# The block sums of the 7-product down chunks on GpSimd, and a seventh such chunk

## The chip, the cores and the metric

The kernel runs on one NeuronCore of a Trainium2 chip. The metric is the device time of one execution in microseconds (us), the median of three runs. All engines that the text names belong to that core: TensorE (PE; its weight loads stand apart as PEld), VectorE (DVE), ScalarE (ACT), GpSimd (POOL) and SyncE (SP), whose queue issues the loads.

## What is computed

One decoder layer for 256 tokens of width 1024: an input projection, two groups of eight attention heads, an output projection, a layer norm, a SwiGLU feed-forward part of inner width 2816, and a second layer norm. The change lies in the last product, the down projection. In the reference:

```
h = _layer_norm(ALPHA * h + mix_out, ln1_g[l], ln1_b[l])
gate = jnp.einsum('bsd,df->bsf', h, w_gate[l])
up = jnp.einsum('bsd,df->bsf', h, w_up[l])
ffn = jnp.einsum('bsf,fd->bsd', jax.nn.silu(gate) * up, w_down[l])
h = _layer_norm(ALPHA * h + ffn, ln2_g[l], ln2_b[l])
```

## The kernel before

Every matmul works on float32 numbers cut in two parts, hi and lo: `split` lets ACT write the rounded hi part and DVE write lo = source - hi. `prod` then issues three matmuls (hi*hi, hi*lo, lo*hi). So each weight has to pass ACT and DVE before PE can use it. Weights come in chunks of 128x2048 (1 MB) through four buffers `wraw`, loaded by SP; the parts lie in five buffers each of `whi` and `wlo` (a pair is called a unit here). `Weights.piece` issues the next piece of this work, and the order on each engine is the order in which the program issues it: an engine that waits holds up all that stands behind it.

The 22 feed-forward tiles (f = 0 to 21) each write a PSUM tile `pg`; after the last of them comes the down projection. It has 11 chunks of two f tiles each, worked through in the order of the table `DOWN`. An ordinary chunk needs one unit, and PE makes 8 products of 512 columns with it (24 matmuls). A chunk in `FAST` is computed as a 2x2 block product with 7 products in place of 8 (21 matmuls), in the manner of Strassen and Winograd. For that it needs two units: A, from the weights as loaded (a 512-column and a 1024-column split), and B, from sums of the weight blocks (two 1024-column splits). The sums are made in place in `wraw` by lines 144, 145 and 146 between the splits of A and those of B: 1024, 512 and 512 columns, each step needing the one before. Of the 7 products the first three use A (PSUM tiles d1, d2, d3), the other four B (d4, d5, d7, d6). The activations of such a chunk need sums of their own (lines 608 to 611, buffer `slots`), and one split of 896 columns.

The last three chunks of `DOWN` are ordinary ones and are worked through in `finish`, token block by token block, so that the layer norm of the first 128 tokens (`layer_norm`, lines 546 to 563, buffer `y`) runs under the matmuls of the second. Ahead of it DVE adds the PSUM tiles of the 7-product chunks together (lines 732 to 743).

Of the kernel before, what the change touches and what calls it, by code (L numbers as in the profile page):

```python
# [10 lines left out]
F32 = mybir.dt.float32  # L11
# [23 lines left out]
NSPLIT = 5  # L35
NWARM = 10

DOWN = (4, 5, 0, 6, 7, 1, 8, 9, 2, 3, 10)
FAST = (4, 5, 6, 7, 8, 9)
ALPHA = 2.0 ** 0.25  # L40
SCALE = DH ** -0.5
LN_EPS = 1e-5
# [5 lines left out]
def decoder_layer(ctx: ExitStack, tc: tile.TileContext, first, x, wqk, wv, wo, wgu, wd,  # L48
                  gmix, lnrows, biases, out):
    nc = tc.nc  # L50
# [24 lines left out]
    def bank(tag, name):  # L75
        return ps.tile([128, 512], F32, tag=tag, name=name)

    def split(src, hi, lo):
        act_e.activation(hi, src, AF.Copy)
        dve.tensor_sub(lo, src, hi)  # L80

    class Weights:
# [51 lines left out]
        def sums(self, c):  # L134

            r = self.raw[c]
            parts = self.parts[c]
            if self.at == 0:
                for k in (slice(0, 512), slice(1024, 2048)):
                    split(r[:, k], parts[0][0][:, k], parts[0][1][:, k])  # L140
                self.at = 512
            elif self.at == 512:
                b = r.rearrange("p (i n) -> p i n", i=4)
                nc.vector.tensor_sub(b[:, 0:2, :], b[:, 1:4:2, :], b[:, 0:2, :])
                nc.vector.tensor_sub(b[:, 3, :], b[:, 3, :], b[:, 0, :])
                nc.vector.tensor_sub(b[:, 2, :], b[:, 2, :], b[:, 3, :])
                self.at = 1024
            else:
                if self.at == 1024:
                    if self.full():  # L150
                        return False
                    parts.append(self.unit())
                o = (self.at - 1024) * 2
                k = slice(o, o + 1024)
                split(r[:, k], parts[1][0][:, k], parts[1][1][:, k])
                self.at += 512
            return True
# [47 lines left out]
    for h in range(2):  # L205
# [3 lines left out]
    weights = Weights([wv[0, 0], wv[0, 1], wqk[0], wqk[1], wv[1, 0], wv[1, 1], wqk[2], wqk[3], wqk[4], wqk[5],  # L209
                       *(wo[c] for c in range(4)), *(wgu[f] for f in range(NFF)), *(wd[c] for c in DOWN)],  # L210
                      [14 + NFF + i for i, c in enumerate(DOWN) if c in FAST])
    weights.load(1)
# [10 lines left out]
    def prod(dst, lhs, rhs, start, stop):  # L223

        pe.matmul(dst, lhs[0], rhs[0], start=start, stop=False, skip_group_check=True)
        pe.matmul(dst, lhs[0], rhs[1], start=False, stop=False, skip_group_check=True)
        pe.matmul(dst, lhs[1], rhs[0], start=False, stop=stop, skip_group_check=True)
# [305 lines left out]
    ff = ctx.enter_context(tc.tile_pool(name="ff", bufs=3, reuse_waits="tile"))  # L533
# [53 lines left out]
    def act_tiles(f):  # L587
        if f < NPAIR:
            act[f] = tuple(cst.tile([128, S], F32R, tag=f"m{f}{i}", name=f"a{i}{f}") for i in range(2))
        else:  # L590
            act[f] = tuple(ff.tile([128, S], F32R, name=f"a{i}{f}", bufs=1) for i in range(2))

    def gated(g, u, shape, tag, dst=None):
        s = ff.tile(shape, F32, tag=tag, name="silu", bufs=3)
        nc.scalar.activation(s, g, AF.Silu)
        if dst is None:
            dst = s
        else:
            s, u = (v.rearrange("p (t n) -> p t n", t=2) for v in (s, u))
        nc.vector.tensor_mul(dst, s, u)  # L600
        return dst


    slots = {}

    def fast_sums(c):
        q = slots.pop(c)
        nc.vector.tensor_add(q[:, 3, :], q[:, 7, :], q[:, 2, :])
        nc.vector.tensor_sub(q[:, 4, :], q[:, 3, :], q[:, 0, :])
        nc.vector.tensor_sub(q[:, 5, :], q[:, 0, :], q[:, 7, :])  # L610
        nc.vector.tensor_sub(q[:, 6, :], q[:, 1, :], q[:, 4, :])  # L611
        fast_act[c] = tuple(ff.tile([128, 7, 128], F32R, name=f"s{i}{c}", bufs=1) for i in range(2))
        split(q[:, 0:7, :], *fast_act[c])
# [21 lines left out]
    def ff_by_channel(f, tag):  # L635
        w = weights.get(14 + f, 1024)
        c, odd = divmod(f, 2)
        fast = c in FAST
        if not fast:
            act_tiles(f)  # L640
        elif not odd:
            slots[c] = ff.tile([128, 8, 128], F32, tag="slots", name="slots", bufs=1)
        p = bank(tag, "pg")
        for half in range(2):
            for kt in range(KT):
                k = slice(kt * 256 + half * 128, kt * 256 + half * 128 + 128)
                od.fill(0.33, lambda: prod(p[:, half * 256:half * 256 + 256], (w[0][:, k], w[1][:, k]),
                                           (xhi[:, kt, :], xlo[:, kt, :]), kt == 0, kt == KT - 1))
        weights.free(14 + f)
        dst = None if not fast else slots[c][:, 1:3, :] if odd else slots[c][:, 0:8:7, :]  # L650
        a = gated(p[:, 0:256], p[:, 256:512], [128, 256], "aw", dst)
        if not fast:
            split(a, *act[f])
        elif odd:
            fast_sums(c)
# [22 lines left out]
    for f in range(NX, NFF):  # L678
        if f == NFF - 8:
            od.pace = 0.9  # L680
        ff_by_channel(f, ("in", "sml")[f % 2])
# [29 lines left out]
    base = 14 + NFF  # L711
    for n, c in enumerate(DOWN[:-nlast]):
        w = weights.get(base + n, 1024)
        if c in FAST:
            sh, sl = fast_act[c]
# [12 lines left out]
    y = ff.tile([128, D], F32, tag="y", name="y", bufs=1)  # L728
# [15 lines left out]

    wl = {c: weights.get(base + len(DOWN) - nlast + n, 1024) for n, c in enumerate(DOWN[-nlast:])}
    pr[9] = bank("big", "d9")
# [82 lines left out]
```

## Time and profile before

| | |
|---|---|
| median of 3 runs | 317.19 us (317.07 to 317.55) |
| profiled execution, its own time | 316.86 us |
| its span, first to last instruction | 315.1 us |
| PE busy | 305.9 us (97%) |
| DVE busy | 240.6 us (76%) |
| ACT busy | 190.7 us (61%) |
| POOL busy | 4.1 us (1%) |
| mean granted TensorE clock | 0.996 |

The span leaves out 1.76 us that lie around it in the profiled execution. Busy shares are means over the whole program; the stage that the change touches is the stretch from about 225 us to 299 us of the span, and the rows further down are taken from there.

### The profile page before, as it was taken

To read this page: it belongs to the slowest core of one execution; us is meant where nothing else is said; L and a number is where in the kernel's file an instruction comes from. 1 tells how busy PE (TensorE), PEld (TensorE's weight loads), DVE (VectorE), ACT (ScalarE), POOL (GpSimd) and SP (SyncE) were. 2 spreads that over 40 slices of the span, in tenths; PEclk is the share of its full clock that TensorE was granted. 3 is DMA by queue.
4 is the path that set the end of the run, shared out by engine and by line. 5 is a ranking of instruction groups with operands and counts; after the bars stand their busy time and mean duration, and the time that the engine had idled before them with its cause. 6 is when DMAs were issued, how large, how long until landed. Compare 5 with 4: busy or idle time off the path is not lost.

```text
span 315.1 us, 5440 instructions
## 1 busy us (share of the span) xinstructions
PE 305.9 (97%) x2112; PEld 277.8 (88%) x2112; DVE 240.6 (76%) x465; ACT 190.7 (61%) x406; POOL 4.1 (1%) x22
## 2 busy tenths in 40 slices
PE   8999999999999999999999999999999999999990
PEld 4988898799997778999999999999999988888880
DVE  4778998659897479997646466585597699999765
ACT  5789997777787458666446364473542675565011
POOL 5000000000000000000000000000000000000000
PEclk9999999999999999999999999999999999999998
DMA  7979887297332104789455464563613253630011
GB/s 255 399 301 381 277 283 263 113 358 292 151 137 69 64 2 133 249 294 370 157 189 214 139 226 172 166 235 133 218 50 136 80 188 130 270 135 0 0 67 67
DMA packets 9657, 58.02 MB, mean 184 GB/s; under 512 B 1184, under 2 KB 1440, under 8 KB 3360
## 3 DMA queue, kind: packets, MB, share of 16 engines
q1 hardware_dynamic: 9344, 57.22, 49.8%
q10 hardware_dynamic: 288, 0.46, 0.4%
q8 instruction: 16, 0.26, 0.3%
q14 instruction: 9, 0.07, 0.1%
HBM read 56.63 MB, written 1.05 MB: 183 GB/s over the span
## 4 chain that ended last, share of the span: by engine, by line
PE 94%; DVE 2%; ACT 1%; DMA 1%; issue 0%; DVEq 0%
PE pg L71 40%; PE p_in L71 22%; PE d L71 15%; PE acc L71 7%; PE z L71 2%; PE o L370 1%; PE s L71 1%; PE warm L185 1%; PE z L311 1%; DVE y L563 1%; PE o L375 1%; DVE bst L548 1%; DMA out_h<-y 1%; DVE y L546 1%; PE o L388 1%; PE tr L575 1%
## 5 line engine op out<-in xcount | busy, mean ns | idle before, releaser
L71 DVE TENSOR_TENSOR wlo<-wraw,whi 128x512 fp32r<-128x512 f32 (+2 forms) x194 | 138.0, 739 | 37.9 <-ACT whi L71 37.0
L71 ACT ACTIVATE whi<-wraw 128x512 fp32r<-128x512 f32 (+2 forms) x194 | 121.2, 671 | 58.0 <-PE pg L71 35.2
L71 PE MATMUL pg<-xhi,whi 128*128 128x256 f32 x304 | 85.7, 282 | 0.0
L71 PE MATMUL pg<-xlo,whi 128*128 128x256 f32 x304 | 85.5, 281 | 0.0
L71 PE MATMUL pg<-xhi,wlo 128*128 128x256 f32 x304 | 85.5, 281 | 0.0
L71 PEld LDWEIGHTS pg<-xhi,whi 128*128 128x128 f32 x304 | 57.2, 188 | 0.0
L71 PEld LDWEIGHTS pg<-xlo,whi 128*128 128x128 f32 x304 | 57.2, 188 | 0.0
L71 PEld LDWEIGHTS pg<-xhi,wlo 128*128 128x128 f32 x304 | 57.2, 188 | 0.0
L71 PE MATMUL p_in<-xhi,whi 128*128 128x256 f32 x128 | 36.5, 286 | 0.0
L71 PE MATMUL p_in<-xhi,wlo 128*128 128x256 f32 x128 | 36.3, 283 | 0.0
L71 PE MATMUL p_in<-xlo,whi 128*128 128x256 f32 x128 | 36.1, 282 | 0.0
L71 PE MATMUL d<-whi,s 128*128 128x512 f32 x84 | 26.9, 395 | 0.0
L71 PE MATMUL d<-whi,a 128*128 128x512 f32 (+1 forms) x92 | 25.9, 363 | 0.0
L71 PEld LDWEIGHTS p_in<-xhi,whi 128*128 128x128 f32 x128 | 24.1, 188 | 1.4 <-issue 0.7
L71 PEld LDWEIGHTS p_in<-xlo,whi 128*128 128x128 f32 x128 | 24.1, 188 | 0.2
L71 PEld LDWEIGHTS p_in<-xhi,wlo 128*128 128x128 f32 x128 | 24.1, 188 | 0.1
L71 PEld LDWEIGHTS d<-whi,s 128*128 128x128 f32 x84 | 15.8, 188 | 3.8
L71 PEld LDWEIGHTS d<-whi,a 128*128 128x128 f32 x92 | 16.6, 189 | 2.9
L71 PE MATMUL d<-wlo,a 128*128 128x512 f32 (+1 forms) x46 | 16.7, 363 | 0.0
L71 PE MATMUL d<-wlo,s 128*128 128x512 f32 x42 | 16.6, 395 | 0.0
L71 ACT ACTIVATE s<-slots 128x896 fp32r<-128x896 f32 x6 | 5.7, 953 | 13.4 <-DVE slots L611 13.4
L71 PE MATMUL pg<-wlo,xhi 128*128 128x256 f32 x48 | 13.6, 286 | 0.0
(151 smaller groups left out, 473.7 us busy)
## 6 DMA issues: line engine op xcount, KB each, us to landing
wraw<-in_wgu SPq DMA_DIRECT2D x22, 1024.0 KB, 4.8
wraw<-in_wd SPq DMA_DIRECT2D x11, 1024.0 KB, 4.8
wraw<-in_wqk SPq DMA_DIRECT2D x6, 1024.0 KB, 5.7
wraw<-in_wo SPq DMA_DIRECT2D x4, 1024.0 KB, 4.7
wraw<-in_first SPq DMA_DIRECT2D x8, 384.0 KB, 6.3
wraw<-in_wv SPq DMA_DIRECT2D x3, 1024.0 KB, 5.4
rows<-in_lnrows SPq DMA_DIRECT2D x2, 1024.0 KB, 6.6
wraw<-in_wv SPq DMA_DIRECT2D x2, 512.0 KB, 7.0
```

Source lines behind the costliest of these rows:

```text
L71: return lambda *a, **k: tc.keep_in_program_order(f(*a, **k)) if Pinned.on else f(*a, **k)
L185: nc.tensor.matmul(warm.rearrange("p (r n) -> p r n", r=4), idle, idle[:, None, :].to_broadcast([128, 4, 128]), start=True, stop=True, ski ...
L311: nc.tensor.matmul(dst, lhs, rhs, start=False, stop=True, skip_group_check=True)
L370: nc.tensor.matmul(o[r, 0:256], vt[g, 0][:, c], w0[:, h * 256:h * 256 + 256], start=True, stop=False, skip_group_check=True)
L375: nc.tensor.matmul(o[r, 128:256], vt[g, 1][:, c], w1[:, h * 128:h * 128 + 128], start=False, stop=True, skip_group_check=True)
L388: nc.tensor.matmul(ms, blkr, sq[:, i, :], start=i == 0, stop=i == 1, skip_group_check=True)
L546: nc.vector.scalar_tensor_tensor(y[:, c], res[:, c], scale, acc[i][:, :c.stop - c.start], op0=ALU.mult, op1=ALU.add)
L548: nc.vector.bn_stats(st[:, i, :], y[:, c])
L563: nc.vector.scalar_tensor_tensor(dst[:, c], y[:, c], r[:, 3:4], b[:, c], op0=ALU.mult, op1=ALU.add)
L575: nc.tensor.transpose(p[:, i * 128:i * 128 + 128], h[:, kt * 128:kt * 128 + 128], ident)
```

## The change

The table of chunks takes one chunk more into the 7-product form (chunk 10, f tiles 20 and 21), and the order of the chunks is another one: the last three are now 1, 2 and 3. The three sums of weight blocks are issued on GpSimd. The buffer in which the activations' sums are made gets the tag of the layer norms' `y`, so that the two share one place.

```diff
-DOWN = (4, 5, 0, 6, 7, 1, 8, 9, 2, 3, 10)
-FAST = (4, 5, 6, 7, 8, 9)
+DOWN = (4, 5, 6, 0, 7, 8, 9, 10, 1, 2, 3)
+FAST = (4, 5, 6, 7, 8, 9, 10)
...
-                nc.vector.tensor_sub(b[:, 0:2, :], b[:, 1:4:2, :], b[:, 0:2, :])
-                nc.vector.tensor_sub(b[:, 3, :], b[:, 3, :], b[:, 0, :])
-                nc.vector.tensor_sub(b[:, 2, :], b[:, 2, :], b[:, 3, :])
+                nc.gpsimd.tensor_sub(b[:, 0:2, :], b[:, 1:4:2, :], b[:, 0:2, :])
+                nc.gpsimd.tensor_sub(b[:, 3, :], b[:, 3, :], b[:, 0, :])
+                nc.gpsimd.tensor_sub(b[:, 2, :], b[:, 2, :], b[:, 3, :])
...
-            slots[c] = ff.tile([128, 8, 128], F32, tag="slots", name="slots", bufs=1)
+            slots[c] = ff.tile([128, 8, 128], F32, tag="y", name="slots", bufs=1)
```

On DVE, at the first 7-product chunk (chunk 4, `wraw_2708`, units `whi_2871` and `whi_2908`), where the feed-forward tiles f = 17 and 18 are still under way:

```order
 L71 TENSOR_TENSOR wlo_2872<-wraw_2708,whi_2871 128x512
 L600 TENSOR_TENSOR slots_2687<-silu_2823,pg_2758 128x256
-L144 TENSOR_TENSOR wraw_2708<-wraw_2708 128x1024
 L608 TENSOR_TENSOR slots_2687<-slots_2687 128x128
 L71 TENSOR_TENSOR wlo_2872<-wraw_2708,whi_2871 128x1024
 L609 TENSOR_TENSOR slots_2687<-slots_2687 128x128
-L145 TENSOR_TENSOR wraw_2708<-wraw_2708 128x512
 L611 TENSOR_TENSOR slots_2687<-slots_2687 128x128
-L146 TENSOR_TENSOR wraw_2708<-wraw_2708 128x512
 L71 TENSOR_TENSOR s18_2831<-slots_2687,s08_2830 128x896
```

The three sums are gone from DVE's order; the splits and the activations' sums stay in the same order.

On POOL, where nothing stood after the constants of the first 5 us, there are now three rows for each of the seven chunks. These are the ones of chunks 7, 8 and 9 (`wraw_2923`, `wraw_3053`, `wraw_3149`):

```order
L144 TENSOR_TENSOR wraw_2923<-wraw_2923 128x1024
L145 TENSOR_TENSOR wraw_2923<-wraw_2923 128x512
L146 TENSOR_TENSOR wraw_2923<-wraw_2923 128x512
L144 TENSOR_TENSOR wraw_3053<-wraw_3053 128x1024
L145 TENSOR_TENSOR wraw_3053<-wraw_3053 128x512
L146 TENSOR_TENSOR wraw_3053<-wraw_3053 128x512
L144 TENSOR_TENSOR wraw_3149<-wraw_3149 128x1024
L145 TENSOR_TENSOR wraw_3149<-wraw_3149 128x512
L146 TENSOR_TENSOR wraw_3149<-wraw_3149 128x512
```

On ACT, in the second half of the down projection. Before, the splits of chunk 8 (`wraw_3139`), chunk 9 (`wraw_3156`) and the ordinary chunk 2 (`wraw_3194`):

```order
L71 ACTIVATE whi_3249<-wraw_3139 128x512
L71 ACTIVATE whi_3249<-wraw_3139 128x1024
L71 ACTIVATE whi_3258<-wraw_3139 128x1024
L71 ACTIVATE whi_3287<-wraw_3156 128x512
L71 ACTIVATE whi_3258<-wraw_3139 128x1024
L71 ACTIVATE whi_3287<-wraw_3156 128x1024
L71 ACTIVATE whi_3296<-wraw_3156 128x1024
```

and now, those of chunk 8 (its end, `wraw_3053`), chunk 9 (`wraw_3149`) and chunk 10 (`wraw_3157`):

```order
L71 ACTIVATE whi_3218<-wraw_3053 128x1024
L71 ACTIVATE whi_3227<-wraw_3053 128x1024 x2
L71 ACTIVATE whi_3259<-wraw_3149 128x512
L71 ACTIVATE whi_3259<-wraw_3149 128x1024
L71 ACTIVATE whi_3289<-wraw_3149 128x1024 x2
L71 ACTIVATE whi_3297<-wraw_3157 128x512
L71 ACTIVATE whi_3297<-wraw_3157 128x1024
L71 ACTIVATE whi_3327<-wraw_3157 128x1024 x2
```

Before, the first piece of chunk 9 stood ahead of the last piece of chunk 8's second unit. Now each chunk's first piece stands behind the last piece of the one before; the same holds for DVE's part of the splits. Only chunks 7 and 8 are still issued in turns.

## Rows read from the trace of the kernel before

**Rows 1.** The page, its span, its engines (1) and its final chain (4).
```profile
span 315.1 us, 5440 instructions
...
PE 305.9 (97%) x2112; PEld 277.8 (88%) x2112; DVE 240.6 (76%) x465; ACT 190.7 (61%) x406; POOL 4.1 (1%) x22
...
PE 94%; DVE 2%; ACT 1%; DMA 1%; issue 0%; DVEq 0%
```
**Rows 2.** Waits of PE, all: who for whom, total us, times, longest.
```profile
PE warm L185 <- DVE idle L182: 1.1, 1, 1.1
PE o L370 <- ACT w L359: 0.2, 1, 0.2
```
**Rows 3.** Windows: length, then each engine's busy us.
```profile
225.00:250.00 25.00, 25.00 (x213) 25.00 (x212) 18.57 (x29) 10.25 (x15) 0.00 (x0) 1.00 0.25 86
250.00:290.00 40.00, 40.00 (x175) 32.41 (x174) 37.95 (x40) 26.49 (x30) 0.00 (x0) 1.00 0.42 158
```
**Rows 4.** Timeline of PE: start, duration; first matmuls of chunks 4, 0 and 6.
```profile
250.04 0.39 PE L71 MATMUL d<-whi,s 128*128 128x512 f32 x1
...
259.83 0.40 PE L71 MATMUL d<-whi,a 128*128 128x512 f32 x1
...
265.30 0.40 PE L71 MATMUL d<-whi,s 128*128 128x512 f32 x1
```
**Rows 5.** Groups by shape on DVE and ACT, 250 to 290 us.
```profile
L71 DVE TENSOR_TENSOR wlo<-wraw,whi 128x1024 fp32r<-128x1024 f32 x22 | 26.0, 1220 | 2.9 <-ACT whi L71 2.8
L144 DVE TENSOR_TENSOR wraw<-wraw 128x1024 f32<-128x1024 f32 x4 | 4.9, 1220 | 0.0
...
L71 DVE TENSOR_TENSOR wlo<-wraw,whi 128x512 fp32r<-128x512 f32 x4 | 2.7, 684 | 0.0
...
L71 ACT ACTIVATE whi<-wraw 128x1024 fp32r<-128x1024 f32 x22 | 22.3, 1053 | 14.3 <-DVE wraw L144 8.2 <-PE pg L71 2.8 <-PE d L71 1.8
L71 ACT ACTIVATE whi<-wraw 128x512 fp32r<-128x512 f32 x4 | 2.5, 625 | 0.0
L683 ACT ACT_TABLE_LOAD x1 | 1.3, 1283 | 0.0
```
**Rows 6.** Window with the activations' sums of one chunk on DVE and ACT.
```profile
238.70:246.10 7.40, 2.36 (x5) 0.95 (x1) 1.00 0.33 134
```
**Rows 7.** Timeline of DVE: the end of the splits and the layer norm's first instructions.
```profile
281.10 9.17 DVE L71 TENSOR_TENSOR wlo<-wraw,whi 128x1024 fp32r<-128x1024 f32 x8
290.18 0.68 DVE L732 SCALAR_TENSOR_TENSOR x_nat<-x_nat,d 128x512 f32<-128x512 f32 x1
290.78 0.68 DVE L736 TENSOR_TENSOR y<-y,d 128x512 f32<-128x512 f32 x1
...
296.15 0.69 DVE L548 BATCH_NORM_STATS2 bst<-y 128x6 f32<-128x512 f32 x1
298.86 0.69 DVE L546 SCALAR_TENSOR_TENSOR y<-x_nat,d 128x512 f32<-128x512 f32 x1 [2.02 <-PE d L71]
```
**Rows 8.** Timeline of POOL, its writes and its copies.
```profile
1.65 0.20 POOL L202 MEMSET negones<- 128x128 f32 x1
1.80 0.29 POOL L201 CAST identb<-ident 128x128 bf16<-128x128 f32 x1
2.04 0.29 POOL L203 TENSOR_SCALAR_AFFINE_SELECT negtri<-negones 128x128 fp32r<-128x128 f32 x1
...
3.28 0.53 POOL L248 MEMSET padlo<- 128x512 f32 x1
3.75 0.53 POOL L247 MEMSET padhi<- 128x512 f32 x1
...
4.78 0.09 POOL L404 MEMSET newton<- 128x1 f32 x1
```
**Rows 9.** Timeline of DVE, its first split, and another one.
```profile
4.82 0.43 DVE L71 TENSOR_TENSOR xlo<-wraw,xhi 128x256 fp32r<-128x256 f32 x1 [3.83 <-ACT xhi L71]
...
5.84 0.42 DVE L71 TENSOR_TENSOR xlo<-wraw,xhi 128x256 fp32r<-128x256 f32 x1
```

## The prediction

> **What bounds the kernel now.** I read the page first. PE is busy for 305.9 of 315.1 us, and the chain that ended last runs 94% on PE [rows 1]. The list of PE's waits says how far that goes: two waits in the whole program, 1.3 us together, both near its start and none in the down projection [rows 2]. So there each matmul follows the last, and the reader is to see how little room there is behind that: in the windows DVE is busy for 37.95 of the 40 us from 250 to 290, ACT for 26.49 and POOL for none [rows 3]. DVE delivers the weights' lo parts only just ahead of PE. The last look is at the tail: DVE's last split ends at 290.2, then it works through its additions, and it waits 2.02 us for PE before the layer norm's instruction at 298.86 [rows 7]. That wait is the slack of the whole chain of splits: a last split that ends more than 2.02 us later than 290.18 delays the layer norm, and with it the end.
>
> **What a 7-product chunk saves.** Chunk 4 starts on PE at 250.04 and the next but one, ordinary chunk 0, at 259.83: two chunks of 21 matmuls take 9.79, one 4.90. Chunk 0 with its 24 takes until 265.30, that is 5.47 [rows 4]. One more 7-product chunk ahead of `finish` thus saves PE 0.57 us (0.18% of the time), and it is the most that the change can bring, because nothing after the chunks becomes shorter: `finish` has three ordinary chunks as before. 0.2%, or 0.63 us, is about what a measurement of this kernel can tell from no change.
>
> **What it takes off DVE.** Six chunks lose 1.22 + 0.68 + 0.68 us of sums on DVE [rows 5] (a 512-column sum costs what the 512-column split does). The new 7-product chunk adds 1536 columns of splits to ACT and DVE. DVE alone becomes less loaded.
>
> **What GpSimd takes for the sums.** No row shows a two-tensor operation on POOL. Its starts bound one [rows 8]: a write of 128 columns takes 0.15 to the next start and one of 512 takes 0.47, so 0.86 ns per column and 0.03 of fixed cost. A copy or select that reads one tensor takes 0.24 for 128 columns, 1.64 ns per column; a second tensor read adds as much again as the first did, which gives 2.4. A chunk has 2048 columns in three instructions: 1.85 us at the pace of a write, 3.45 at that of a copy, 5.0 with two reads. I take 4.5, between the copy and the two reads and nearer to the two reads, because a subtraction has two. That is 1.9 us longer than on DVE, and the three sums depend on each other, so nothing divides them. A sentence by itself: the Trainium skill (GPSIMD Engine Reference, section 3.1) gives 4497 ns for a two-tensor operation of 2048 columns, by which the estimate would be the same 4.5.
>
> **Who waits for them.** ACT's splits for unit B wait for the sums, behind these on ACT stand the next chunk's first split, and behind their DVE halves the next chunk's too; PE waits at the fourth product of a chunk (d4, the first from B). Once chunks 9 and 10 are reached, no piece of the next chunk lies ahead of the last piece of the current one, so the whole round lies on the path. The loads are not late: a raw buffer is free when the chunk four before it is split (chunk 6 for chunk 9), some 20 us ahead. The shared buffer of `y` and `slots` costs nothing: the first norm has let go of it long before tile f = 8, and the second's `y` is wanted only after the last split. Chunk 10's activations add a split of 0.95 on ACT and 2.36 of busy time on DVE [rows 6] just after 250 us, in place of ordinary splits.
>
> **Whether the two engines work at the same time.** This decides the size. The one place in the trace where they meet is at 4.8 us: a DVE split of two tensors in SBUF took 0.43 while POOL's last writes ran, against 0.42 a little later [rows 8, 9]. But there POOL only wrote; that it may read two tensors while DVE also reads two is shown nowhere. I cost both ends: side by side without loss, and strictly in turns. I take the turns, the nearer to what the change asks of them (both read the very same `wraw` tile, chunk by chunk), and keep the other for the range. Weighed against the trace: the Trainium skill (SBUF — State Buffer, section "Who interferes with whom") says that a DVE instruction with two SBUF inputs contends with a GpSimd instruction that reads SBUF, not with one that only writes, and that the later one blocks until the first is done. By that rule the turns hold and the time is the 333.5 below; the rows at 4.8 us agree with its second half, and no row here shows the first.
>
> **The sum, in turns.** Starts on DVE lie 0.08 before the last end (eight splits of 1.22 in 9.17 [rows 7]), so a 1024-column split counts 1.14, a 512-column one 0.60, and the activations' five 1.94. Unit A of chunk 6 can start when the last feed-forward tile is done, at 250.04 [rows 4]; ACT's half takes 0.63 [rows 5], and DVE, with the end of chunk 5's split still to do, reaches it at about 252.0. From there DVE has five 7-product chunks (0.60 + 3 x 1.14 = 4.02 each, 20.1), chunk 10's activations (1.9) and four ordinary chunks (8 x 1.14 = 9.1): 31.1. POOL has five chunks of 4.5: 22.5. In turns that is 53.6. In chunks 6, 9 and 10 neither has anything to do while ACT splits the last block, 1.05 [rows 5] each: 3.2. The last split ends at 252.0 + 53.6 + 3.2 = 308.8, which is 18.6 after 290.18; less the slack of 2.02 the layer norm starts 16.6 later. The saving of 0.57 doesn't count then, since DVE sets the end. 316.86 + 16.6 = **333.5 us** for an execution like the profiled one. The median of the runs lay 0.33 above that one, so I forecast **333.8**. At 5.0 for a chunk's sums, with bubbles in chunks 7 and 8 too, it would be 338; at 3.45 some 328.
>
> **Rivals.** *Side by side* (slower too, by less). Chunk 6's sums end at 256.1; ACT then does in order a block of 1.05, the activations' 0.95, the table load of 1.28, chunk 0's two blocks and chunk 7's first [rows 5, 6], with DVE 1.8 behind: 263.6. The sums of chunks 7 and 8 follow one another, until 273.3. A round of chunk 9 or 10 is ACT 1.05, DVE 1.14 and 0.69, the sums 4.5 and some 0.2 of hand-over: 7.6, against the 4.90 that PE needs. 288.5, then 1.05 and seven splits of 1.14: 297.6, 7.4 late, 5.4 over the slack: 322.3, with the 0.33 322.6. For it: DVE's own load falls, and nothing in the trace shows the two engines in each other's way. *Part of each*, a DVE that only slows down while POOL reads: between 323 and 333.
>
> *Hidden* (the other side). If the two work side by side and a chunk's sums cost little, the splits stay ahead of PE and only the 0.57 remains: 316.6 by the median. Four chunks' sums (7 to 10) lie on the chain, so it decides at 4.5 - (5.4 + 0.6) / 4 = 3.0 us a chunk, below what the copies' pace gives (3.45) and above that of the writes (1.85). Against it speaks that a subtraction reads more than a copy does.
>
> **How the numbers follow.** In turns 0.50; side by side 0.27; part of each 0.13; hidden 0.10. The range leaves out the hidden case, the dearest turns and the cheapest of side by side: 321 to 337.5. Hidden lands at -0.18%, within 0.2% more often than beyond it: faster 0.03, same 0.08, slower 0.89.
>
> **What would show it.** In the profile after: PE waits in the down projection, on the splits' `whi` and `wlo`, growing from chunk 7 on and largest at the fourth product of chunks 9 and 10; ACT's idle time ahead of `whi` released by POOL's `wraw`; POOL starts of L144 and L145 some 2.2 and 1.1 apart. In turns, DVE's 1024-column splits that meet a sum last longer than 1.22 (or sums longer than 2.3), and hardly a moment has both busy to the full; side by side they keep their 1.22. DVE goes straight from its last split into the additions and no longer waits 2.02 ahead of L546. The forecast is wrong if PE has no waits there, if the splits keep 1.22 under the sums, or if L144 on POOL is far from 2.2.

## The result and the profile after

The changed kernel takes 336.06 us (median of 4 runs, 335.90 to 336.14) against 317.25 us for the kernel before (median of 4, 317.07 to 317.55): a ratio of 1.0592, 95% interval 1.0578 to 1.0605. It is 18.8 us slower. The forecast was 333.8 with a range of 321 to 337.5. The time alone doesn't say whether the two engines worked in turns; the rows do.

The page of the kernel after, its span and busy times:

```profile
span 334.4 us, 5467 instructions
...
PE 311.6 (93%) x2109; PEld 280.2 (84%) x2109; DVE 242.1 (72%) x452; ACT 192.5 (58%) x407; POOL 46.0 (14%) x43
```

Against [rows 1] the span has grown by 19.3 us. DVE lost 13 instructions and is busy for longer. That is the first sign: part of what is counted as busy there must be something else.

PE's waits after, from 225 us on (who for whom, total us, times, longest). In [rows 2] there was none in this stretch.

```profile
PE d L71 <- ACT whi L71: 8.0, 3, 3.7
PE d L71 <- DVE wlo L71: 4.5, 4, 2.5
```

The timeline of POOL after (start, duration): the sums of chunk 4, those of chunk 9 and the first of chunk 10.

```profile
229.27 2.39 POOL L144 TENSOR_TENSOR wraw<-wraw 128x1024 f32<-128x1024 f32 x1 [224.39 <-DVE wlo L71]
233.09 1.28 POOL L145 TENSOR_TENSOR wraw<-wraw 128x512 f32<-128x512 f32 x1 [1.43 <-DVE wlo L71]
234.45 1.30 POOL L146 TENSOR_TENSOR wraw<-wraw 128x512 f32<-128x512 f32 x1
...
285.73 3.32 POOL L144 TENSOR_TENSOR wraw<-wraw 128x1024 f32<-128x1024 f32 x1 [3.03 <-DVE wlo L71]
289.13 1.29 POOL L145 TENSOR_TENSOR wraw<-wraw 128x512 f32<-128x512 f32 x1
290.49 2.12 POOL L146 TENSOR_TENSOR wraw<-wraw 128x512 f32<-128x512 f32 x1
295.65 3.29 POOL L144 TENSOR_TENSOR wraw<-wraw 128x1024 f32<-128x1024 f32 x1 [3.03 <-DVE wlo L71]
```

And the timeline of DVE after, at the same places and at the end of the splits:

```profile
229.55 2.25 DVE L608 TENSOR_TENSOR slots<-slots 128x128 f32<-128x128 f32 x1
231.73 1.21 DVE L71 TENSOR_TENSOR wlo<-wraw,whi 128x1024 fp32r<-128x1024 f32 x1
232.87 0.28 DVE L609 TENSOR_TENSOR slots<-slots 128x128 f32<-128x128 f32 x1
...
283.83 2.96 DVE L71 TENSOR_TENSOR wlo<-wraw,whi 128x1024 fp32r<-128x1024 f32 x3 [3.64 <-ACT whi L71]
290.18 1.32 DVE L71 TENSOR_TENSOR wlo<-wraw,whi 128x1024 fp32r<-128x1024 f32 x1 [3.39 <-ACT whi L71]
293.74 2.96 DVE L71 TENSOR_TENSOR wlo<-wraw,whi 128x1024 fp32r<-128x1024 f32 x3 [2.24 <-ACT whi L71]
...
303.62 8.03 DVE L71 TENSOR_TENSOR wlo<-wraw,whi 128x1024 fp32r<-128x1024 f32 x7 [2.24 <-ACT whi L71]
311.58 0.68 DVE L732 SCALAR_TENSOR_TENSOR x_nat<-x_nat,d 128x512 f32<-128x512 f32 x1
...
318.15 0.67 DVE L546 SCALAR_TENSOR_TENSOR y<-x_nat,d 128x512 f32<-128x512 f32 x1
```

The two lists are to be read side by side.

*DVE waits for POOL.* L608 adds 128 columns. Its neighbour L609, of the same shape, takes 0.28 at 232.87. L608 starts at 229.55, while POOL's L144 runs (229.27 to 231.66), and ends at 231.80, a moment after it. Nothing connects the two: L608 reads activations, L144 weights. The time for which it was held up is counted in its duration, not as idle time.

*POOL waits for DVE.* L144 takes 2.39 at 229.27, alone, and 3.32 at 285.73. There DVE's last of three splits was under way, from 285.57 (286.79 less its 1.22), and ended 1.06 after L144's start. L146 takes 2.12 at 290.49, under the split of 290.18, in place of 1.29.

So whichever starts second stands until the first is done, in both directions. The Trainium skill (SBUF — State Buffer, section "Who interferes with whom") states it so, for a DVE instruction with two SBUF inputs against a GpSimd one that reads SBUF; these rows agree. L600, one of whose inputs (`pg`) lies in PSUM, is not held up: at 240.49 it takes 0.41, as before, and L144, which starts under it at 240.65, takes its 2.39.

*The round.* From L144 of chunk 9 to that of chunk 10 pass 9.92 us (285.73 to 295.65), where PE needs 4.90 for such a chunk [rows 4]. They divide so: the three sums until 292.61; ACT's last block until 293.7; DVE's splits until 295.57. ACT's timeline after, in that round:

```profile
289.08 1.06 ACT L71 ACTIVATE whi<-wraw 128x1024 fp32r<-128x1024 f32 x1 [3.82 <-POOL wraw L144]
292.65 2.52 ACT L71 ACTIVATE whi<-wraw 128x1024 fp32r<-128x1024 f32 x3 [2.50 <-POOL wraw L146]
```

The row of 292.65 holds chunk 9's last block and, behind it, the first pieces of chunk 10. They don't need the sums, but stand behind them in ACT's order, so nothing of the next chunk overlaps with the sums of this one.

*The end.* The last split ends where L732 starts, at 311.58 against 290.18 [rows 7]. L546 at 318.15 no longer waits. 311.58 - 290.18 - 2.02 = 19.4: the whole growth of the span.

### The profile page after: what moved, and what is told of

Same layout as the page of the kernel before. It is cut to its first block, busy times and chain, and to the rows that moved or that the text cites. A ratio compares the mean times of both kernels' runs of the same rounds, so it can differ in the third digit from the quotient of the medians.

```text
span 334.4 us, 5467 instructions
## 1 busy us (share of the span) xinstructions
PE 311.6 (93%) x2109; PEld 280.2 (84%) x2109; DVE 242.1 (72%) x452; ACT 192.5 (58%) x407; POOL 46.0 (14%) x43
## 3 DMA queue, kind: packets, MB, share of 16 engines
HBM read 56.63 MB, written 1.05 MB: 172 GB/s over the span
## 4 chain that ended last, share of the span: by engine, by line
PE 69%; DVE 11%; POOL 8%; ACT 4%; DMA 4%; issue 2%; POOLq 1%; DVEq 0%; ACTq 0%
PE pg L71 37%; PE p_in L71 17%; PE acc L71 7%; DVE wlo L71 5%; POOL wraw L144 3%; POOL wraw L145 2%; DMA wraw<-in_wv 2%; POOL wraw L146 2%; ACT whi L71 2%; PE z L71 2%; PE o L370 1%; PE s L71 1%; PE z L311 1%; DMA wraw<-in_first 1%; DVE bst L548 1%
## 5 line engine op out<-in xcount | busy, mean ns | idle before, releaser
L71 DVE TENSOR_TENSOR wlo<-wraw,whi 128x512 fp32r<-128x512 f32 (+2 forms) x196 | 142.9, 757 | 57.0 <-ACT whi L71 56.2
L71 ACT ACTIVATE whi<-wraw 128x512 fp32r<-128x512 f32 (+2 forms) x196 | 122.9, 672 | 74.9 <-PE pg L71 32.5
L144 POOL TENSOR_TENSOR wraw<-wraw 128x1024 f32<-128x1024 f32 x7 | 19.4, 2777 | 248.3 <-DVE wlo L71 248.3
L71 PE MATMUL d<-whi,s 128*128 128x512 f32 x98 | 34.8, 431 | 8.0 <-ACT whi L71 8.0
L71 PEld LDWEIGHTS d<-whi,s 128*128 128x128 f32 x98 | 20.7, 211 | 14.2 <-ACT whi L71 9.3
L71 PE MATMUL d<-wlo,s 128*128 128x512 f32 x49 | 21.9, 446 | 4.5 <-DVE wlo L71 4.5
L71 PE MATMUL d<-whi,a 128*128 128x512 f32 (+1 forms) x76 | 20.7, 356 | 0.0
L71 PEld LDWEIGHTS d<-wlo,s 128*128 128x128 f32 x49 | 10.3, 211 | 8.3 <-DVE wlo L71 5.9
L71 ACT ACTIVATE s<-slots 128x896 fp32r<-128x896 f32 x7 | 6.7, 951 | 16.4 <-DVE slots L611 16.4
L71 PEld LDWEIGHTS d<-whi,a 128*128 128x128 f32 x76 | 13.6, 189 | 2.1
```

Source lines behind the costliest of these rows:

```text
L71: return lambda *a, **k: tc.keep_in_program_order(f(*a, **k)) if Pinned.on else f(*a, **k)
L144: nc.gpsimd.tensor_sub(b[:, 0:2, :], b[:, 1:4:2, :], b[:, 0:2, :])
```

## The experiments

Two things had to be settled: how much of the 18.8 us comes from GpSimd at all, and whether that share is the sums' greater length, or that the two engines exclude each other. Each ratio is to the kernel before, in runs on the same chip (medians 317.17 in the first set, e1, e2, e4 and e6, and 317.53 in the second), with its 95% interval.

**e1_seven_on_dve**: the changed kernel with the sums back on DVE.

```diff
-                nc.gpsimd.tensor_sub(b[:, 0:2, :], b[:, 1:4:2, :], b[:, 0:2, :])
-                nc.gpsimd.tensor_sub(b[:, 3, :], b[:, 3, :], b[:, 0, :])
-                nc.gpsimd.tensor_sub(b[:, 2, :], b[:, 2, :], b[:, 3, :])
+                nc.vector.tensor_sub(b[:, 0:2, :], b[:, 1:4:2, :], b[:, 0:2, :])
+                nc.vector.tensor_sub(b[:, 3, :], b[:, 3, :], b[:, 0, :])
+                nc.vector.tensor_sub(b[:, 2, :], b[:, 2, :], b[:, 3, :])
```

> The change with the block sums back on DVE (the seventh 7-product chunk, the new order and the shared buffer stay). If the loss comes from GpSimd (its length and the turns), nearly all of it goes: DVE has one 7-product chunk more (4.0 of splits, 2.6 of sums and 1.9 for the activations in place of 2.3 and 0.7, so some 5.5 us more work, less the idle time it has before 250 us and the 2.0 of slack), 1.5 to 3.5 us above the kernel before, 318.7 to 320.7. The rival, that the new order and the extra chunk by themselves break the flow of the splits, expects it near the changed kernel, 330 or more.

Measured 319.88, ratio 1.0084 (1.0069 to 1.0099). PE has no wait in the down projection, as before, and still the kernel is slower. The timeline of DVE in this kernel shows why:

```profile
286.46 9.17 DVE L71 TENSOR_TENSOR wlo<-wraw,whi 128x1024 fp32r<-128x1024 f32 x8
295.55 0.68 DVE L732 SCALAR_TENSOR_TENSOR x_nat<-x_nat,d 128x512 f32<-128x512 f32 x1
...
302.12 0.67 DVE L546 SCALAR_TENSOR_TENSOR y<-x_nat,d 128x512 f32<-128x512 f32 x1
```

The seventh chunk gives DVE more to split and add. Its last split ends 5.37 us after that of before [rows 7]; less the slack of 2.02 that is 3.35, and the span grew by 3.3. The seventh chunk with its order costs 2.7 by the medians; the other 16 us need GpSimd. They hold a change of order too: in e1 ACT and DVE still take the first piece of chunk 9 ahead of the last piece of chunk 8, and that of chunk 10 ahead of the last of chunk 9, which the change does not.

**e2_six_on_pool**: the kernel before, with only lines 144 to 146 on GpSimd.

```diff
-                nc.vector.tensor_sub(b[:, 0:2, :], b[:, 1:4:2, :], b[:, 0:2, :])
-                nc.vector.tensor_sub(b[:, 3, :], b[:, 3, :], b[:, 0, :])
-                nc.vector.tensor_sub(b[:, 2, :], b[:, 2, :], b[:, 3, :])
+                nc.gpsimd.tensor_sub(b[:, 0:2, :], b[:, 1:4:2, :], b[:, 0:2, :])
+                nc.gpsimd.tensor_sub(b[:, 3, :], b[:, 3, :], b[:, 0, :])
+                nc.gpsimd.tensor_sub(b[:, 2, :], b[:, 2, :], b[:, 3, :])
```

> The kernel before with nothing changed but the engine of the block sums: six chunks, the old order. In turns: POOL's 5.0 us for each of chunks 6 to 9 come on top of DVE's splits, 20 us in place of the 10.5 that the sums took on DVE, and ACT's wait after the last sum of some chunks: 8 to 13 us above before, 325 to 330. Side by side, where only the sums' length counts: in the old order the next chunk's first pieces lie ahead of the last pieces, so only about 2 us, 318 to 320.

Measured 327.15, ratio 1.0311 (1.0294 to 1.0328): 10.0 us, in the range of turns. The groups by shape on DVE from 250 to 312 us (count, busy us and mean ns, idle time ahead) show the splits lengthened from 1220 and 684 ns [rows 5]:

```profile
L71 DVE TENSOR_TENSOR wlo<-wraw,whi 128x1024 fp32r<-128x1024 f32 x23 | 33.3, 1476 | 15.2 <-ACT whi L71 15.1
L71 DVE TENSOR_TENSOR wlo<-wraw,whi 128x512 fp32r<-128x512 f32 x4 | 3.8, 958 | 0.0
```

But the order did not stay the old one. Before, ACT took the first piece of chunk 9 ahead of the last piece of chunk 8; here its row of 283.42 holds chunk 8's last block and, behind it, the first pieces of chunk 9, as in the change, though the program differs from before in the engine alone. So the order on an engine is not simply the one in which the program issues the work, as the section on the kernel before has it. PE's wait at chunk 9 in this kernel is as long as in the change. ACT's row and PE's:

```profile
283.42 2.53 ACT L71 ACTIVATE whi<-wraw 128x1024 fp32r<-128x1024 f32 x3 [2.54 <-POOL wraw L146]
...
294.44 0.50 PE L71 MATMUL d<-whi,s 128*128 128x512 f32 x1 [3.72 <-ACT whi L71]
```

The two parts alone cost 2.7 and 10.0, 12.7 together; the change costs 18.8. The change has a fifth set of sums behind 250 us, and two rounds (chunks 9 and 10) that can't overlap where e2 has one. I put the 6.1 us over the sum down to that; it is argued, and no run divides them further.

**e6_bystander**: the kernel before, its sums still on DVE. For each 7-product chunk GpSimd makes three subtractions more, of 1024, 512 and 512 columns, into a tile that nobody reads. The tag of `slots` is that of the change, to make room.

```diff
+                a = parts[0][0].bitcast(F32)
+                xs = xhi.rearrange("p k n -> p (k n)").bitcast(F32)
+                for o, n in ((0, 1024), (1024, 512), (1536, 512)):
+                    nc.gpsimd.tensor_sub(self.scratch[:, :n], a[:, 1024:1024 + n], xs[:, o:o + n])
...
+    weights.scratch = ff.tile([128, 1024], F32, name="scratch", bufs=1)
```

> The kernel before (sums on DVE, six chunks) with three extra subtractions on GpSimd for each 7-product chunk, of 1024, 512 and 512 columns, from two tensors in SBUF into a scratch tile that nobody reads; slots lie in the buffer of the norms to make room. No engine waits for their result. Turns: each of them holds DVE's splits up, 5.0 us a chunk in chunks 6 to 9, so some 20 us less DVE's idle 2 and its slack of 2: 12 to 18 us above before, 329 to 335. Side by side: within 0.5 us of before, 317.

Measured 337.03, ratio 1.0625 (1.0599 to 1.0652): 19.9 us for work on which no one depends. The list of waits names POOL as no one's releaser; still DVE's instructions lengthened. Groups by shape on DVE, 250 to 312 us, in this kernel (L148 is line 144 of the other kernels):

```profile
L71 DVE TENSOR_TENSOR wlo<-wraw,whi 128x1024 fp32r<-128x1024 f32 x24 | 37.1, 1583 | 0.0
L148 DVE TENSOR_TENSOR wraw<-wraw 128x1024 f32<-128x1024 f32 x4 | 7.1, 1765 | 0.0
```

This separates the exclusion from the chain of dependences: here no split waits for a sum on GpSimd, and the order on DVE is that of before, so each instruction can be set against the same one there. From the timeline of DVE before, the last sum of chunk 5 and the first of chunk 6:

```profile
243.81 0.68 DVE L146 TENSOR_TENSOR wraw<-wraw 128x512 f32<-128x512 f32 x1
...
254.87 1.22 DVE L144 TENSOR_TENSOR wraw<-wraw 128x1024 f32<-128x1024 f32 x1
```

The same two in this kernel, its first addition behind the splits (L737 is L732) and the layer norm (L551 is L546):

```profile
250.52 0.68 DVE L150 TENSOR_TENSOR wraw<-wraw 128x512 f32<-128x512 f32 x1
...
259.22 1.23 DVE L148 TENSOR_TENSOR wraw<-wraw 128x1024 f32<-128x1024 f32 x1
...
310.89 0.68 DVE L737 SCALAR_TENSOR_TENSOR x_nat<-x_nat,d 128x512 f32<-128x512 f32 x1
...
317.87 0.69 DVE L551 SCALAR_TENSOR_TENSOR y<-x_nat,d 128x512 f32<-128x512 f32 x1 [0.32 <-PE d L71]
```

The time came out above the 12 to 18 us expected, which had left out chunks 4 and 5. At the end of chunk 5 DVE is 6.7 late; its idle time takes 2.4 off that, so that chunk 6 starts 4.35 late. Chunks 6 to 9 then add 17.1, about 4.3 each (not 5.0), and idle time takes off another 0.7. The last split ends 20.7 late; less 2.02 that is 18.7. L546 still waits 0.32 for PE, so it starts 19.0 late, and the span grew by 19.1.

**e4_pool_writes**: the changed kernel with plain writes on GpSimd in place of the sums, 5504 columns a chunk in nine pieces, made to last about as long. The weights' sums are left out, and the second unit holds zeros.

```diff
-                nc.gpsimd.tensor_sub(b[:, 0:2, :], b[:, 1:4:2, :], b[:, 0:2, :])
-                nc.gpsimd.tensor_sub(b[:, 3, :], b[:, 3, :], b[:, 0, :])
-                nc.gpsimd.tensor_sub(b[:, 2, :], b[:, 2, :], b[:, 3, :])
+                for n in (1024, 1024, 640):
+                    nc.gpsimd.memset(r[:, 0:n], 0.0)
+                for n in (512, 512, 384):
+                    nc.gpsimd.memset(r[:, 1536:1536 + n], 0.0)
+                for n in (512, 512, 384):
+                    nc.gpsimd.memset(r[:, 1024:1024 + n], 0.0)
```

> The change with each block sum replaced by three memsets of about the same total time on GpSimd (2688 and twice 1408 columns at 0.86 ns), at the same place with the same waits; the weights' sums are left out, so the second unit holds zeros. POOL is as long on the path, but reads nothing. If it is the reading that blocks DVE, the splits keep 1.22 us under POOL's work and the time is that of side by side with 5.0 us a chunk, 323 to 327. If the length of the sums in the chain alone made the loss, it stays near 336. If writes block DVE as well, it stays there too, and then DVE's short sums at L608 last over 2 us again, which tells the two apart.

Measured 318.96, ratio 1.0054 (1.0038 to 1.0070), below the expectation. DVE's splits keep 1220 ns under the writes (groups by shape on DVE, 250 to 312 us):

```profile
L71 DVE TENSOR_TENSOR wlo<-wraw,whi 128x1024 fp32r<-128x1024 f32 x23 | 27.0, 1220 | 10.1 <-ACT whi L71 10.1
```

But by itself the run is inconclusive: with the writes the order on ACT and DVE came out differently, the next chunk's first pieces ahead of the last piece of the current one. Part of the difference to 336.06 is the order. So a pair was run with one order for both:

**e7_pinned** and **e8_pinned_writes**: the changed kernel, and e4, each with the splits of the 7-product chunks held in the program's order on ACT and DVE. In e8 the weights' sums are left out, as in e4.

```diff
+    def split_in_order(src, hi, lo):
+        tc.keep_in_program_order(nc.scalar.activation(hi, src, AF.Copy))
+        tc.keep_in_program_order(nc.vector.tensor_sub(lo, src, hi))
...
-                    split(r[:, k], parts[0][0][:, k], parts[0][1][:, k])
+                    split_in_order(r[:, k], parts[0][0][:, k], parts[0][1][:, k])
...
-                split(r[:, k], parts[1][0][:, k], parts[1][1][:, k])
+                split_in_order(r[:, k], parts[1][0][:, k], parts[1][1][:, k])
```

> The changed kernel with the splits of the 7-product chunks on ACT and DVE held to the order in which the program writes them, so that chunk 8's first pieces too stand behind chunk 7's last. It is the base for the next run, whose order is the same. One round more on the path than in the changed kernel: 336 to 341.

> The run before with the three sums of a chunk replaced by memsets on GpSimd of about the same total time (5.2 us a chunk, 5.0 for the sums free of DVE), in the same order on ACT and DVE; the weights' sums are left out. If reading two tensors is what blocks DVE, only the length stays on the path: a round of some 7.8 us against 4.9 of PE in chunks 7 to 10, 8 to 12 us above before, 325 to 330, and DVE's 128-column sums under POOL's work last 0.29. If the length alone made the loss, within 2 us of the run before.

e7 took 340.40, ratio 1.0735 (1.0714 to 1.0757); e8 took 327.89, ratio 1.0332 (1.0317 to 1.0348). The timeline and the groups by shape (250 to 312 us) of DVE in e7, L612 being L608 of the other kernels:

```profile
229.67 2.27 DVE L612 TENSOR_TENSOR slots<-slots 128x128 f32<-128x128 f32 x1
...
L84 DVE TENSOR_TENSOR wlo<-wraw,whi 128x1024 fp32r<-128x1024 f32 x16 | 22.1, 1380 | 25.1 <-ACT whi L83 25.0
```

The same views of e8, where the same instruction is L615:

```profile
229.41 0.29 DVE L615 TENSOR_TENSOR slots<-slots 128x128 f32<-128x128 f32 x1
...
L84 DVE TENSOR_TENSOR wlo<-wraw,whi 128x1024 fp32r<-128x1024 f32 x16 | 19.6, 1223 | 17.1 <-ACT whi L83 17.1
```

With writes that keep POOL as long (5.25 us a chunk in e8, 274.15 to 279.40, against 4.96 for the sums) DVE is not held up at all: 0.29 against 2.27, 1223 against 1380. The pair differs by 12.5 us. That is what reading on GpSimd costs in this order; the other 10.4, e8 against the kernel before, are the seventh chunk, the order and the length of the chain. The change's own order has no such pair, so its 16 us are not divided in this way.

**e5_two_on_pool**: the kernel before, with the sums of its first two 7-product chunks alone (4 and 5) on GpSimd.

```diff
-                nc.vector.tensor_sub(b[:, 0:2, :], b[:, 1:4:2, :], b[:, 0:2, :])
-                nc.vector.tensor_sub(b[:, 3, :], b[:, 3, :], b[:, 0, :])
-                nc.vector.tensor_sub(b[:, 2, :], b[:, 2, :], b[:, 3, :])
+                (nc.gpsimd if c < 14 + NFF + 2 else nc.vector).tensor_sub(b[:, 0:2, :], b[:, 1:4:2, :], b[:, 0:2, :])
+                (nc.gpsimd if c < 14 + NFF + 2 else nc.vector).tensor_sub(b[:, 3, :], b[:, 3, :], b[:, 0, :])
+                (nc.gpsimd if c < 14 + NFF + 2 else nc.vector).tensor_sub(b[:, 2, :], b[:, 2, :], b[:, 3, :])
```

> The kernel before with the sums of its first two 7-product chunks (4 and 5) on GpSimd, the other four on DVE. These two are made under the feed-forward matmuls, where DVE has idle time (18.6 of 25 us busy). In turns DVE's 128-column sum at L608 lasts over 2 us there, but all of it is hidden: within 0.2% of before, 316.6 to 317.8. If a sum on GpSimd cost something wherever it stands, two chunks of six would give a third of the six-chunk run's 10 us, 320.

Measured 317.44, ratio 1.0002 (0.9993 to 1.0011): nothing. DVE's timeline in this kernel shows the same hold-up as after:

```profile
229.97 2.25 DVE L608 TENSOR_TENSOR slots<-slots 128x128 f32<-128x128 f32 x1
```

But there the feed-forward tiles still run on PE, DVE has idle time (18.57 of 25 us busy [rows 3]), and PE has no wait. So the first two chunks' sums are free on GpSimd, and the cost comes from the chunks behind them. DVE gives its own sums away here. In e6, which leaves them on DVE, the subtractions of the same two chunks were not free: chunk 6 started 4.35 late.

**e3_y_only**: the kernel before, with only the tag of `slots` changed.

```diff
-            slots[c] = ff.tile([128, 8, 128], F32, tag="slots", name="slots", bufs=1)
+            slots[c] = ff.tile([128, 8, 128], F32, tag="y", name="slots", bufs=1)
```

> The kernel before with nothing changed but the place of the activations' sums (the buffer of the norms). Nothing waits for that buffer: within 0.2% of before, 316.6 to 317.8. If the shared buffer made somebody wait, slower by a microsecond or more.

Measured 317.60, ratio 1.0001 (0.9993 to 1.0010): the shared buffer costs nothing.

## Why the prediction was right

**The mechanism.** In turns was forecast at 0.50. The rows after, e6 and the pair e7 and e8 show it: an exclusion by whole instructions, in both directions, between DVE's operations on two SBUF tensors and GpSimd's subtractions, also without any dependence. *Side by side* and *part of each* fall with it. The reasons given for the turns were weaker than the outcome. That both engines read the very same `wraw` tile is not what counts, since L608 and L144 share none; and the rows at 4.8 us, which were to agree on the writes, overlap by only 0.05 (4.82 to 4.87). It was e8 that showed the writes harmless.

**The step that was mis-sized** is "I take 4.5" for a chunk's sums. Undisturbed, as at 229.27, they take 2.39 + 1.28 + 1.30 = 4.97, the upper bound of the prediction. The rows also say why: 512 columns more cost 2.39 - 1.28 = 1.11, or 2.17 ns per column, so 2048 take 4.44; what is missing is 0.17 of fixed cost for each of three instructions, of which I had only counted the 0.03 of the writes. The Trainium skill (GPSIMD Engine Reference, section 3.1) gives 4497 ns for 2048 columns in one operation, by estimate 2.2 ns per column; the rows agree on the pace, and the figure says nothing of three small operations.

Five chunks at 0.47 more give 2.4 of the 2.8 us by which the last split came later than forecast (311.58 against 308.8). That the two are so close is partly luck, because other terms were off and cancel. The stretches in which both engines stand while ACT works were put at three of 1.05, 3.2 together. They were four of 1.12 (chunk 8 has one too, from 282.70 to 283.83) and one of 0.98 ahead of DVE's split at 263.92, which waits for ACT behind the table load: 5.5, 2.3 more. Against that DVE began chunk 6's first split at 251.28 and not at 252.0, and some 1.2 are gained where the engines meet: an instruction that has stood ends sooner after the other than by its whole own time (L608 0.14 after L144, where it takes 0.28 alone; L146 of chunk 9 1.11 after DVE's split, where it takes 1.29). The 1.2 are what is left over, and no run divides them. A round shows the same: 9.92 against 4.5 + 4.02 + 1.05 = 9.6, with sums 0.47 longer, ACT's block 0.07 longer, and 0.2 gained.

PE also waits 0.5 ahead of the stage, at a `p_in` matmul for DVE's `ol`, which the trace of before doesn't have. Waits of 0.3 to 0.4 at `p_in`, there on ACT's `whi`, stand in the traces of e2, e4 and e5 too, so I take it for chance; no run tests that.

Two sums in the prediction are inexact, without weight. The starts of 0.15 and 0.47 give 0.83 ns per column and 0.04 of fixed cost for a write, not 0.86 and 0.03. In side by side, chunk 6's sums end at 257.1 when counted from the 252.0 of the sum in turns (with 0.60 and 4.5), not at 256.1, and 263.6 with two sums is 272.6, not 273.3; together they move its 322.6 by 0.3.

**The slack.** "Delays the layer norm, and with it the end" held exactly in the kernel after (19.4 worked out, 19.3 measured) and in e1 (3.35 and 3.3), where L546 waits for PE no longer. In e6 and e2 it still waits, 0.32 and 0.64 us, and starts 19.0 and 10.8 later than before, where the splits alone give 18.7 and 10.2. There PE, late by its own waits, sets the rest. DVE's timeline in e2:

```profile
302.38 0.68 DVE L732 SCALAR_TENSOR_TENSOR x_nat<-x_nat,d 128x512 f32<-128x512 f32 x1
...
309.67 0.69 DVE L546 SCALAR_TENSOR_TENSOR y<-x_nat,d 128x512 f32<-128x512 f32 x1 [0.64 <-PE d L71]
```

**The waits of PE** came at the fourth product, where forecast. But they don't simply grow: the first, of chunk 7, is one of the two largest. The timeline of PE after, the waits of chunks 7 (two rows), 9 and 10:

```profile
275.00 0.50 PE L71 MATMUL d<-whi,s 128*128 128x512 f32 x1 [2.04 <-ACT whi L71]
277.98 0.80 PE L71 MATMUL d<-wlo,s 128*128 128x512 f32 x1 [2.48 <-DVE wlo L71]
...
293.76 0.50 PE L71 MATMUL d<-whi,s 128*128 128x512 f32 x1 [3.72 <-ACT whi L71]
...
303.64 0.50 PE L71 MATMUL d<-whi,s 128*128 128x512 f32 x1 [2.22 <-ACT whi L71]
```

The 2.48 of chunk 7 is DVE's last split held up by chunk 8's L144. The rows of POOL and of DVE after (the first of DVE's three splits is chunk 7's last; it ends at 277.92):

```profile
274.49 2.35 POOL L144 TENSOR_TENSOR wraw<-wraw 128x1024 f32<-128x1024 f32 x1 [0.63 <-DVE wlo L71]
...
274.98 5.21 DVE L71 TENSOR_TENSOR wlo<-wraw,whi 128x1024 fp32r<-128x1024 f32 x3 [0.57 <-ACT whi L71]
```

This is an instance of the turns in which the sums of the next chunk delay the current one. That the sums of chunks 7 and 8 are issued in turns did not protect them.

**Hidden** needed sums below 3.0 us a chunk that hold up nobody. Neither is so. Without the hold-up, a chain of 5.25 us gave 319.0 in the looser order (e4) and 327.9 in the strict one (e8), on both sides of the 322.6 worked out for side by side. So the order, which I had taken as fixed, is worth some 9 us between these two.

**A sign that was read too simply.** "Hardly a moment has both busy to the full" can't be read from busy times, because an instruction that is held up counts as busy. The windows after, 250 to 290 us (length; PE, PEld, DVE, ACT, POOL; granted clock; share of the DMA engines, GB/s):

```profile
250.00:290.00 40.00, 34.98 (x144) 27.16 (x143) 25.44 (x23) 17.66 (x20) 22.72 (x11) 0.96 0.37 132
```

DVE and POOL add to 48.2 of 40 us, although one of them stood whenever their two-tensor work met. The lengthened means and the single rows tell it, not the shares.

## What to carry to other kernels

Moving an elementwise subtraction from DVE to GpSimd added no second engine here while DVE itself worked on pairs of SBUF tensors: the times nearly add up, and GpSimd takes 1.9 times as long (4.96 us for a chunk's sums against 2.58 on DVE). It was free where DVE had idle time and PE waited for none of it, as in e5. Look for the hold-up in durations, not in waits: the same shape with two durations is the trace of it (0.28 and 2.25, 2.39 and 3.32). And a kernel whose PE never waits may still be bound by another engine's chain: read the wait at the end of that chain (2.02 us here) before giving it more work (e1). Last, moving an operation can change the order of others (e2, e4); hold the order fixed, as in e7 and e8, before a difference is put down to the engine.

## What was not expected of the hardware

PE's own pace was lower behind its longest waits. Windows of the kernel after, before, in and behind the wait of chunk 9 (columns as above):

```profile
285.00:290.00 5.00, 4.89 (x20) 3.69 (x20) 1.79 (x3) 1.18 (x2) 4.19 (x2) 1.00 0.55 210
290.00:295.00 5.00, 0.53 (x2) 0.19 (x1) 2.58 (x3) 2.50 (x4) 2.54 (x2) 0.99 0.00 0
295.00:300.00 5.00, 4.98 (x15) 3.99 (x16) 1.70 (x2) 1.21 (x2) 4.28 (x2) 0.67 0.56 215
```

The timeline of PE after, ahead of that wait and behind it:

```profile
288.24 0.63 PE L71 MATMUL d<-whi,s 128*128 128x512 f32 x2
...
288.94 0.63 PE L71 MATMUL d<-whi,s 128*128 128x512 f32 x2
...
295.61 1.05 PE L71 MATMUL d<-whi,s 128*128 128x512 f32 x2
...
296.89 1.05 PE L71 MATMUL d<-whi,s 128*128 128x512 f32 x2
```

At a granted clock of 1.00 (2.4 GHz) a product of three matmuls takes 0.70 (288.24 to 288.94); after 0.53 us of work in five it takes 1.28 (295.61 to 296.89), and the window has 0.67, a mean between that level and the lower one, 1.2 GHz. From 298.2 on the pace is the old one. Over the whole span PE's busy time rose by 5.7 us (305.9 [rows 1] to 311.6) with three matmuls fewer, and with 12.5 us of waits from 225 us on that makes 18.2 of the 19.3. It did not set the end here, since L546 waits for PE no longer. In e2, e6 and e7 it still waits 0.64, 0.32 and 0.39, so there a late PE set the end by that much.
